# A two-layer decoder trunk: streamed sums placed more thinly in the first MLP, negated scores with an undivided first map, and one head-norm chain for both token tiles

## The chip, the core and the metric

One core of a Trainium2 chip runs the whole program. The metric is the device time of one execution in microseconds, as the median of three runs. The engines are named as the profile names them: PE is TensorE (PEld its weight loads), DVE is VectorE, ACT is ScalarE, POOL is GpSimd, SP is SyncE, whose queue issues the streamed loads.

## The reference, cut to what matters

A sequence of 256 tokens with 1024 features passes two layers, all in float32. Each layer is a token mixer and a squared-ReLU MLP with 4096 hidden columns; both are normed before, and shift, scale and gate of each norm come from a conditioning vector `c` (one product of `c` with a 1024 x 6144 matrix per layer). The mixer of layer 0 is native sparse attention (16 heads, three branches with gates), that of layer 1 is differential attention (8 heads with two maps each).

```python
cond = jax.nn.silu(c)
for i in range(DEPTH):
    mod = cond @ w_ada[i] + b_ada[i]
    sh1, sc1, g1, sh2, sc2, g2 = jnp.split(mod, 6, axis=-1)
    h = rms_norm(x, ln_mix_g[i]) * (1.0 + sc1[:, None, :]) + sh1[:, None, :]
    y = nsa_mixer(h, ...) if i % 2 == 0 else diff_mixer(h, ...)
    x = x + g1[:, None, :] * y
    h = rms_norm(x, ln_mlp_g[i]) * (1.0 + sc2[:, None, :]) + sh2[:, None, :]
    x = x + g2[:, None, :] * (jnp.square(jax.nn.relu(h @ w_mlp_in[i])) @ w_mlp_out[i])

# diff_mixer, for every head; q and k after a norm over 64 columns and a rotation of the first 16
q = apply_partial_rope(rms_norm(q, q_gain), cos, sin)
k = apply_partial_rope(rms_norm(k, k_gain), cos, sin)
s = jnp.einsum('bhcqd,bhckd->bhcqk', qb, k) * scale        # two maps c, scale = 1/8
p = masked_softmax(s, kpos[None, :] <= t[:, None])
a = p[:, :, 0] - lam * p[:, :, 1]
o = jnp.einsum('bhqk,bhkd->bhqd', a, v)
o = rms_norm(o, subln_g) * (1.0 - lam_init)                # over 128 columns
```

## The kernel before, in words

**Products.** Every large product is made of exactly split operands: `w = hi + lo`, both in float32r, and `mm3` (L79 to L83) adds hi.hi, hi.lo and lo.hi in one bank of 512 columns. A 256 x 1024 activation stands as two token tiles of 128.

**The weight stream.** Before anything is computed, the program writes two lists: `items` (raw buffers of 128 x 1024 floats, 524 KB each, loaded by SP in that order) and `units` (what is to be done with them). `plan` (L112) appends a unit of weights; `plan_ada` (L118) appends eight steps of a conditioning sum, one for each tile of 128 rows of the conditioning matrix. `do_unit` (L187) takes the units in their order. A weight unit is split: a cast for the high half (L199) on the engine that the table `halves` names for this turn, and a subtraction for the low half (L203) on the other. A conditioning step is one operation on VectorE over 1024 columns: a multiplication for the first of eight (L224), then a multiply-add (L229); with `with_pool` (second MLP only) VectorE multiplies (L226) and GpSimd adds (L227). `use` (L238) does the units up to the next weights and splits `look` units ahead; `issue` (L154) starts loads `ahead_dma` items ahead. Raw buffers, halves, sums and larger activations share one ring of 32 slots of 4 KB a partition (tag "w").

**Where the sums stand.** `plan_mlp` (L517) writes the units of an MLP with its extra steps: from the third block on one step behind every unit, until there are none. The first MLP carries 24 steps: its own gate, and shift and scale of the differential layer's norm. Shift and scale of the second MLP's norm, 16 steps, stand in the differential layer: `one_k` (L556) puts one behind each of the first 16 units of the projections q0, k1, q1 and v0. The second MLP carries 8 steps for its gate. After the eighth step `fin` folds a sum over partitions: `ada_cols` (L362) with four small products (L366), a copy, and, as an entry of the list `pend`, two transposes and a copy (L374, L376). `flush` (L183) runs all of `pend` at the next weight unit. `fin_gate` (L413) folds a gate by products at once.

**Head norms.** `head_norms` (L792) takes the two token tiles of a projection as they lie in their banks. For each tile: squares on ScalarE (L798), sums of 64 columns on VectorE (L800), then `rsqrt_mean` (L299): a small VectorE operation (L302), logarithm and exponential on ScalarE (L306, L307), and four small VectorE operations for a Newton step (L308 to L311). Then the multiplication (L811), the rotation `rope` (L782: two products L788, a difference L789, a sum L790), four transposes on TensorE (L826), and ScalarE's copies with the gain into the key tiles (L842) or the query tile (L849). It is a generator; at each `yield fill` `weave` (L252) puts `fill` units of the next projection's products behind it. In `kv_post` (L893) the two key kinds of the sparse layer go through it one after the other.

**Attention.** `mask_max` (L1005) adds a mask of 0 and a large negative number and takes the maximum in one VectorE operation (L1008). A small operation multiplies the maximum by -0.125 (L1023 in the sparse layer, L1349 in the other), and ScalarE takes `exp(0.125 s + bias)` with its sum (L1028, L1354). `combine` (L1357) of the differential layer divides: a reciprocal, the second one times -lambda, then for each token tile a scaling of the first map (L1361) and a multiply-add of the second (L1362). Transposes (L1368), values (L1375, L1377), a norm over 128 columns, transposes (L1390) and the split (L1392, L1393) follow, head by head, in the order that the string given to `heads` (L1397) spells out (L1430 to L1437).

**Order.** The program text gives an order, which the framework's scheduler may change engine by engine; the splits and the sums are issued with a lowered priority (`tc.high_priority(-50)`), and semaphores between the engines are set by the framework. So the rows of the orders below are what each engine's queue holds.

## Time and profile before

| | |
|---|---|
| median of three runs | 747.58 us (745.33 to 747.91) |
| span of the profiled execution (the page gives no other time for it) | 746.7 us |
| TensorE busy | 692.4 us (93%), 4263 products and transposes |
| VectorE busy | 505.6 us (68%) |
| ScalarE busy | 385.5 us (52%) |
| GpSimd busy | 233.5 us (31%) |
| read from memory | 154.86 MB, 209 GB/s over the span |

The program runs through stretches that the lines of the trace set apart: the start and first norm (0 to 62 us), the sparse layer (62 to 212, from 185 on mostly its output projection and the next norm), the first MLP (212 to 405), the differential layer (405 to 572, from 546 on mostly the end of its output projection and the next norm), the second MLP (572 to 747). Shares over the whole span mix these, so they are read stretch by stretch. A group of instructions is shown with its line, engine, operation, tiles (out<-in, partitions x elements), count, busy time and mean time of one.

### The profile page before, as it was taken

How to read it: one execution, taken by the hardware profiler on the slowest of the kernel's cores; microseconds unless marked ns; L12 is line 12 of the kernel's file. 1: busy time of each engine (PE TensorE's matmuls, PEld its weight loads, DVE VectorE, ACT ScalarE, POOL GpSimd, SP SyncE). 2: the span in 40 equal slices, each digit the busy share in tenths (PEclk: the TensorE clock that was granted, in tenths of full speed). 3: DMA queues.
4: the chain of work that ended last, by engine and by line, in shares of the span. 5: the costliest groups of instructions: out<-in, count | busy, mean ns of one | idle time of the engine just before them, and what ended most of it. 6: DMA issues, size and time to landing. Idle time of an engine off the chain costs nothing. (4 is left out here: it accounts for less than half of the span.)

```text
span 746.7 us, 11822 instructions
## 1 busy us (share of the span) xinstructions
PE 692.4 (93%) x4263; PEld 569.3 (76%) x4263; DVE 505.6 (68%) x1051; ACT 385.5 (52%) x780; POOL 233.5 (31%) x151
## 2 busy tenths in 40 slices
PE   8999799998889999999999978888889999999997
PEld 6788565665578988899885756566669879988896
DVE  4447989969766788764338969888777653326653
ACT  6555338667356345554447342666646365445540
POOL 4102800004222232232324413125322864223430
PEclk9999999999999999999999989899999999999999
DMA  9999999313636999965676776434383499565001
GB/s 292 333 337 358 321 296 270 117 57 119 198 107 197 329 312 334 350 208 186 200 246 232 257 225 224 148 104 117 111 281 112 145 314 331 173 206 183 5 1 57
DMA packets 105423, 156.70 MB, mean 210 GB/s; under 512 B 6135, under 2 KB 60180, under 8 KB 105364
## 3 DMA queue, kind: packets, MB, share of 16 engines
q1 hardware_dynamic: 103952, 153.60, 64.0%
q0 software_dynamic: 1248, 2.20, 1.0%
q8 instruction: 34, 0.56, 0.3%
q14 instruction: 25, 0.20, 0.1%
q10 hardware_dynamic: 164, 0.14, 0.1%
HBM read 154.86 MB, written 1.06 MB: 209 GB/s over the span
## 5 line engine op out<-in xcount | busy, mean ns | idle before, releaser
L203 POOL TENSOR_TENSOR wl<-wr,wh 128x1024 fp32r<-128x1024 f32 x66 | 171.1, 2593 | 371.7 <-ACT wh L199 273.4
L203 DVE TENSOR_TENSOR wl<-wr,wh 128x1024 fp32r<-128x1024 f32 x126 | 181.2, 1451 | 80.4 <-ACT wh L199 49.9
L199 ACT CAST wh<-wr 128x1024 fp32r<-128x1024 f32 (+1 forms) x175 | 174.9, 1029 | 51.5 <-POOL acc L227 16.1
L83 PE MATMUL acc<-wh,z 128*128 128x512 f32 (+1 forms) x320 | 126.5, 396 | 5.2 <-DVE z L77 4.7
L81 PE MATMUL acc<-wh,z 128*128 128x512 f32 (+1 forms) x320 | 127.9, 400 | 0.0
L82 PE MATMUL acc<-wl,z 128*128 128x512 f32 (+1 forms) x320 | 126.2, 394 | 0.0
L83 PE MATMUL sc<-hh,wl 128*128 128x256 f32 x384 | 108.9, 284 | 1.2 <-POOL wl L203 1.2
L81 PE MATMUL sc<-hh,wh 128*128 128x256 f32 x384 | 109.2, 284 | 0.0
L82 PE MATMUL sc<-hl,wh 128*128 128x256 f32 x384 | 108.8, 283 | 0.0
L81 PEld LDWEIGHTS sc<-hh,wh 128*128 128x128 f32 x384 | 73.7, 192 | 2.1 <-issue 1.2
L83 PEld LDWEIGHTS sc<-hh,wl 128*128 128x128 f32 x384 | 73.7, 192 | 1.4 <-POOL wl L203 1.4
L83 PEld LDWEIGHTS acc<-wh,z 128*128 128x128 f32 x320 | 60.5, 189 | 18.5 <-DVE z L77 5.6
L82 PEld LDWEIGHTS sc<-hl,wh 128*128 128x128 f32 x384 | 73.7, 192 | 0.5
L1199 ACT ACTIVATE t<-sc 128x512 f32<-128x512 f32 x32 | 19.1, 597 | 101.1 <-PE sc L83 101.0
L81 PEld LDWEIGHTS acc<-wh,z 128*128 128x128 f32 x320 | 60.7, 190 | 12.4 <-issue 0.9
L82 PEld LDWEIGHTS acc<-wl,z 128*128 128x128 f32 x320 | 60.6, 189 | 11.9 <-issue 0.7
L77 DVE TENSOR_TENSOR z<-t,z 128x512 fp32r<-128x512 f32 x24 | 24.5, 1020 | 66.6 <-ACT z L76 66.5
L81 PE MATMUL acc<-wh,hh 128*128 128x512 f32 (+1 forms) x160 | 66.2, 415 | 2.1 <-DVE qn L811 1.3
L229 DVE SCALAR_TENSOR_TENSOR acc<-wr,cond,acc 128x1024 f32<-128x1024 f32 x42 | 62.7, 1493 | 0.6
L83 PE MATMUL acc<-wh,hl 128*128 128x512 f32 (+1 forms) x160 | 62.3, 389 | 0.6 <-DVE hl L1161 0.6
L82 PE MATMUL acc<-wl,hh 128*128 128x512 f32 (+1 forms) x160 | 62.3, 389 | 0.5 <-DVE wl L203 0.5
L81 PE MATMUL sc<-wh,hh 128*128 128x256 f32 (+1 forms) x152 | 44.1, 292 | 1.4 <-DVE hh L1160 1.4
(292 smaller groups left out, 1202.5 us busy)
## 6 DMA issues: line engine op xcount, KB each, us to landing
wr<-in_w_ada_dram SPq DMA_DIRECT2D x80, 512.0 KB, 6.5
wr<-in_w_mlp_in_dram SPq DMA_DIRECT2D x64, 512.0 KB, 5.0
wr<-in_w_mlp_out_dram SPq DMA_DIRECT2D x64, 512.0 KB, 4.4
wr<-in_diff_w_in_dram SPq DMA_DIRECT2D x24, 512.0 KB, 4.9
wr<-in_w_ada_dram SPq DMA_DIRECT2D x32, 256.0 KB, 6.6
wr<-in_nsa_w_in_dram SPq DMA_DIRECT2D x16, 512.0 KB, 7.4
wr<-in_nsa_w_out_dram SPq DMA_DIRECT2D x16, 256.0 KB, 10.8
wr<-in_diff_w_out_dram SPq DMA_DIRECT2D x8, 512.0 KB, 3.6
```

What stands on the lines that cost most here:

```text
L77: vec.tensor_tensor(l, src, h.bitcast(F32), op=ALU.subtract)
L81: pe.matmul(out, x[0], w[0], start=start, stop=False, skip_group_check=True)
L82: pe.matmul(out, x[0], w[1], start=False, stop=False, skip_group_check=True)
L83: pe.matmul(out, x[1], w[0], start=False, stop=stop, skip_group_check=True)
L199: hi(h, r[:, 0:n])
L203: lo.tensor_tensor(l, r[:, 0:n], h.bitcast(F32), op=ALU.subtract)
L229: vec.scalar_tensor_tensor(st["acc"], r, c, st["acc"], op0=ALU.mult, op1=ALU.add)
L1199: act.activation(r, bk, AF.Relu)
```

## The change

1. *Sums.* `plan_mlp` gets a function `share(i)` that gives the steps behind unit i. The first MLP carries all 40 steps: its gate, and shift and scale of the next two norms, one behind each of three of four units from the tenth on (`i > 7` and `i % 4 > 0`, i from 0). The projections of the differential layer carry none. The second MLP has its 8 steps behind the units from the thirteenth on, one each.
2. *Folding.* Entries of `pend` have a count. `ada_cols` queues its products three weight units later and the transposes one unit after them; `fin_gate` is queued three units later too.
3. *Head norms.* One chain for both token tiles: the sums of squares go into one 128 x 16 tile, and `rsqrt_mean` and `rope` run once over both tiles; the multiplications stay one for each tile. The normed heads lie in one slot of the ring (`w4`) instead of two small tiles. In the sparse layer's `kv_post` the two key kinds go through one chain too, and the gate sums stand inside it. For keys of the differential layer the last of the three fills is two units instead of one.
4. *Negated scores.* The gains of the queries are multiplied by -0.125 once, so products of queries and keys are the negated, scaled scores; the mask is 0 and a large positive number, the operation takes the minimum, and the exponential is `exp(-s + min)`. The small operation in between is left out.
5. *Undivided first map.* `combine` leaves the first map as it is and adds the second times -lambda s0 / s1. Since a norm over columns follows, the factor s0 is left out but for EPS, which becomes EPS s0 s0.
6. *Halves.* In the differential layer all high halves are cast by ScalarE; every second low half is made by GpSimd, as before.

```diff
-    def flush():
-        while pend:
-            pend.pop(0)()
+    def flush(everything=True):
+        for e in pend:
+            e[0] -= 1
+        while pend and (everything or pend[0][0] <= 0):
+            pend.pop(0)[1]()
...
     def ada_cols(acc, then):
-        bk = bank()
...
+        def front():
+            bk = bank()
...
+            act.copy(row, bk[:, 0:256])
+            pend.insert(0, [1, lambda: back(row)])
...
-        pend.append(back)
+        pend.append([3, front])
...
-        return f
+        return lambda acc: pend.append([3, lambda: f(acc)])
...
+        for j in (0, 3):
+            vec.tensor_scalar(grot[:, j : j + 1], grot[:, j : j + 1], -0.125, None, op0=ALU.mult)
...
+    def head_norms(blocks, tabs, finish, perm=False, plain=None, fill=(1, 1, 1)):
+        ss = small([P, 2, 8], "hns")
+        q = w4("qn").rearrange("p (t h d) -> p t h d", t=2, h=8)
+        for t, hs, b in blocks:
+            n = hs.stop - hs.start
+            sq = tmp()[:, 0 : 64 * n]
             act.activation(sq, b, AF.Square)
-            ss = small([P, 8], "hns")[:, 0:nh]
-            vec.reduce_sum(ss, sq.rearrange("p (h d) -> p h d", d=64), axis=AX.X)
-            rs.append(rsqrt_mean(ss, 64, [P, nh], f"hn{nh}"))
-        yield fill
+            vec.reduce_sum(ss[:, t, hs], sq.rearrange("p (h d) -> p h d", d=64), axis=AX.X)
+        r = rsqrt_mean(ss.rearrange("p t h -> p (t h)"), 64, [P, 16], "hn").rearrange("p (t h) -> p t h", t=2)
+        yield fill[0]
...
+        rope(q, tabs)
+        yield fill[2]
+        heads_T(q, finish)
...
-    def mask_max(bks, pr, mx):
+    def mask_min(bks, pr, mn):
...
-                vec.tensor_tensor_reduce(pr[:, h, T2[t][1]], bk[:, h * w : (h + 1) * w], m, 1.0, -3e38, ALU.add, ALU.max,
-                                         mx(h, t))
+                vec.tensor_tensor_reduce(pr[:, h, T2[t][1]], bk[:, h * w : (h + 1) * w], m, 1.0, 3e38, ALU.add, ALU.min,
+                                         mn(h, t))
...
-    plan_mlp(0, [(0, 1, 2), (1, 0, 0), (1, 0, 1)])
+    plan_mlp(0, [(0, 1, 2), (1, 0, 0), (1, 0, 1), (1, 1, 0), (1, 1, 1)], lambda i: int(i % 4 > 0) if i > 7 else 0)
...
-        U["d" + nm, i] = plan_rows(w_dif, c0, [[one_k]] * 4)
+        U["d" + nm, i] = plan_rows(w_dif, c0)
...
-    plan_mlp(1, [(1, 1, 2, True)])
+    plan_mlp(1, [(1, 1, 2, True)], lambda i: int(i > 11))
...
-    halves[0] = [(vec.tensor_copy, pool), (act.copy, vec), (act.copy, pool), (act.copy, vec)]
+    halves[0] = [(act.copy, pool), (act.copy, vec)]
...
         def combine(s):
-            vec.reciprocal(s.sm, s.sm)
-            vec.tensor_scalar(s.sm[:, :, 1], s.sm[:, :, 1], nlam, None, op0=ALU.mult)
+            r, e = s.cf[:, 0], s.cf[:, 1]
+            vec.reciprocal(r, s.sm[:, 1])
+            vec.scalar_tensor_tensor(r, r, nlam, s.sm[:, 0], op0=ALU.mult, op1=ALU.mult)
+            vec.scalar_tensor_tensor(e, s.sm[:, 0], EPS, s.sm[:, 0], op0=ALU.mult, op1=ALU.mult)
             for t, sl in T2:
-                vec.tensor_scalar(s.pr[:, 0, sl], s.pr[:, 0, sl], s.sm[:, t, 0:1], None, op0=ALU.mult)
-                vec.scalar_tensor_tensor(s.pr[:, 0, sl], s.pr[:, 1, sl], s.sm[:, t, 1:2], s.pr[:, 0, sl],
+                vec.scalar_tensor_tensor(s.pr[:, 0, sl], s.pr[:, 1, sl], r[:, t : t + 1], s.pr[:, 0, sl],
                                          op0=ALU.mult, op1=ALU.add)
...
-    weave(head_norms(bk0, 4, 8, to_kz(4, kz[0:2])), gq)
+    weave(head_norms(rows8(bk0), [(slice(0, 8), 4)], to_kz((4, 4), kz[0:2]), fill=(1, 1, 2)), gq)
...
-    c[:, 264:392] = np.where(p[None, :] <= p[:, None], 0.0, NEG)
+    c[:, 264:392] = np.where(p[None, :] <= p[:, None], 0.0, -NEG)
```

What this does to the order of the queues is shown at three places. The first is VectorE at the first key norm of the differential layer; `hn8t`, `hn8r` and `hn8m` are the small tiles of the norm (`hnt`, `hnr`, `hnm` in the changed kernel), `wl` is the low half of a weight unit, `acc` of L229 a conditioning sum. Before:

```order
L229 SCALAR_TENSOR_TENSOR acc<-wr,cond,acc 128x1024
L310 TENSOR_SCALAR hn8t<-hn8t 128x8
L309 TENSOR_TENSOR hn8t<-hn8t,hn8m 128x8
L229 SCALAR_TENSOR_TENSOR acc<-wr,cond,acc 128x1024
L311 TENSOR_TENSOR hn8r<-hn8r,hn8t 128x8
L310 TENSOR_SCALAR hn8t<-hn8t 128x8
L229 SCALAR_TENSOR_TENSOR acc<-wr,cond,acc 128x1024
L311 TENSOR_TENSOR hn8r<-hn8r,hn8t 128x8
L811 TENSOR_TENSOR qn<-acc,hn8r 128x512 x2
L788 TENSOR_TENSOR ropeA<-qn,csg 128x128
L788 TENSOR_TENSOR ropeB<-qn,csg 128x128
L203 TENSOR_TENSOR wl<-wr,wh 128x1024
```

In the changed kernel:

```order
L805 TENSOR_REDUCE hns<-t 128x8
L305 TENSOR_SCALAR hnm<-hns 128x16
L308 TENSOR_TENSOR hnt<-hnr 128x16
L309 TENSOR_TENSOR hnt<-hnt,hnm 128x16
L310 TENSOR_SCALAR hnt<-hnt 128x16
L311 TENSOR_TENSOR hnr<-hnr,hnt 128x16
L814 TENSOR_TENSOR qn<-acc,hnr 128x512 x2
L781 TENSOR_TENSOR ropeA<-qn,csg 128x256
L781 TENSOR_TENSOR ropeB<-qn,csg 128x256
L206 TENSOR_TENSOR wl<-wr,wh 128x1024
L784 TENSOR_TENSOR qn<-ropeA,ropeB 128x16x8
L785 TENSOR_TENSOR qn<-ropeA,ropeB 128x16x8
```

The three conditioning sums that stood between the small operations are no longer in the queue, a norm has one chain of small operations instead of two interleaved ones, and the rotary products have 256 columns.

The second place is TensorE at the same norm, with buffer numbers: `acc_4571` and `acc_4572` are the two banks of the q0 projection, `acc_4728` and `acc_4729` those of k1, and L826 are the transposes behind the norm. Before:

```order
L82 MATMUL acc_4571<-wl_4509,hh_138 128x512
L826 MATMUL tr_4680<-first_75,qn_4622 128x128 x4
L83 MATMUL acc_4571<-wh_4508,hl_139 128x512
L81 MATMUL acc_4572<-wh_4508,hh_138 128x512
L82 MATMUL acc_4572<-wl_4509,hh_138 128x512
L83 MATMUL acc_4572<-wh_4508,hl_139 128x512
L81 MATMUL acc_4728<-wh_4603,hh_138 128x512
L82 MATMUL acc_4728<-wl_4604,hh_138 128x512
L83 MATMUL acc_4728<-wh_4603,hl_139 128x512
L81 MATMUL acc_4729<-wh_4603,hh_138 128x512
L82 MATMUL acc_4729<-wl_4604,hh_138 128x512
L826 MATMUL tr_4689<-first_75,qn_4624 128x128 x4
```

In the changed kernel `acc_4507` and `acc_4508` are the banks of q0, `acc_4623` and `acc_4624` those of k1, and the transposes are L793:

```order
L83 MATMUL acc_4507<-wh_4447,hl_139 128x512
L81 MATMUL acc_4508<-wh_4447,hh_138 128x512
L82 MATMUL acc_4508<-wl_4448,hh_138 128x512
L83 MATMUL acc_4508<-wh_4447,hl_139 128x512
L793 MATMUL tr_4603<-first_75,qn_4510 128x128 x4
L793 MATMUL tr_4612<-first_75,qn_4510 128x128 x4
L81 MATMUL acc_4623<-wh_4527,hh_138 128x512
L82 MATMUL acc_4623<-wl_4528,hh_138 128x512
L83 MATMUL acc_4623<-wh_4527,hl_139 128x512
L81 MATMUL acc_4624<-wh_4527,hh_138 128x512
```

The transposes of the first tile stood ahead of the last four products of q0, and those of the second tile behind five products of k1. Now all 48 products of q0 stand ahead, and the transposes of both tiles follow one another.

The third place is VectorE in the last blocks of the first MLP, where `z` is the low half of a hidden block (L77) and `acs` the folded columns of a sum. Before:

```order
L77 TENSOR_TENSOR z_3850<-t,z_3849 128x512
L203 TENSOR_TENSOR wl<-wr,wh 128x1024 x3
L77 TENSOR_TENSOR z_3850<-t,z_3849 128x512
L203 TENSOR_TENSOR wl<-wr,wh 128x1024 x2
L77 TENSOR_TENSOR z_4058<-t,z_4057 128x512
L203 TENSOR_TENSOR wl<-wr,wh 128x1024 x3
L77 TENSOR_TENSOR z_4058<-t,z_4057 128x512
```

In the changed kernel (L206 is the low half, L227 and L232 the conditioning steps, L378 the copy of the folded columns):

```order
L77 TENSOR_TENSOR z_3737<-t,z_3736 128x512
L206 TENSOR_TENSOR wl<-wr,wh 128x1024
L227 TENSOR_SCALAR acc<-wr,cond 128x1024
L77 TENSOR_TENSOR z_3737<-t,z_3736 128x512
L232 SCALAR_TENSOR_TENSOR acc<-wr,cond,acc 128x1024 x2
L378 COPY acs<-tr 128x2x4
L206 TENSOR_TENSOR wl<-wr,wh 128x1024
L387 TENSOR_TENSOR mB_136<-acs,bcol 128x8
L206 TENSOR_TENSOR wl<-wr,wh 128x1024
L232 SCALAR_TENSOR_TENSOR acc<-wr,cond,acc 128x1024 x4
L206 TENSOR_TENSOR wl<-wr,wh 128x1024
L232 SCALAR_TENSOR_TENSOR acc<-wr,cond,acc 128x1024
```

The steps for the second MLP's shift and scale stand between the low halves here.

## Rows read from the trace of the kernel before

**Rows 1.** Busy time by stretch (x: instructions)

```profile
core 0: us, PE busy (x) PEld busy (x) DVE busy (x) ACT busy (x) POOL busy (x), PEclk, DMA share, GB/s
...
62.00:100.00 38.00, 31.43 (x192) 23.88 (x191) 34.00 (x84) 16.59 (x45) 18.46 (x21) 0.96 1.06 318
100.00:185.00 85.00, 81.04 (x501) 50.25 (x500) 73.46 (x336) 58.32 (x195) 10.25 (x4) 0.98 0.57 162
...
212.00:405.00 193.00, 188.98 (x1223) 168.25 (x1223) 122.23 (x108) 94.85 (x129) 54.96 (x28) 0.99 0.75 251
405.00:480.00 75.00, 63.91 (x270) 47.63 (x271) 66.03 (x132) 33.34 (x71) 25.50 (x16) 0.91 0.65 217
480.00:546.00 66.00, 57.23 (x271) 42.09 (x269) 53.41 (x171) 40.50 (x129) 24.71 (x17) 0.97 0.38 116
...
572.00:747.00 175.00, 169.00 (x1076) 153.09 (x1074) 85.02 (x67) 79.10 (x99) 69.31 (x28) 1.00 0.47 157
```

**Rows 2.** Waits of TensorE, 405 to 546 us (total us, times, longest us)

```profile
PE tr L826 <- DVE qn L790: 10.9, 4, 4.2
PE tr L1368 <- DVE z L1393: 2.2, 2, 1.6
```

**Rows 3.** Timeline of TensorE, 430 to 436 us (start us, us, [idle before])

```profile
430.59 0.39 PE L81 MATMUL acc<-wh,hh 128*128 128x512 f32 x1
430.82 0.39 PE L82 MATMUL acc<-wl,hh 128*128 128x512 f32 x1
435.20 1.12 PE L826 MATMUL tr<-first,qn 128*128 128x128 f32 x4 [3.99 <-DVE qn L790]
```

**Rows 4.** Timeline of ScalarE and VectorE, 419 to 434 us

```profile
419.51 0.60 ACT L798 ACTIVATE t<-acc 128x512 f32<-128x512 f32 x1 [5.39 <-PE acc L83]
...
427.07 2.38 DVE L310 TENSOR_SCALAR hn8t<-hn8t 128x8 f32<-128x8 f32 x1
...
429.44 1.28 DVE L229 SCALAR_TENSOR_TENSOR acc<-wr,cond,acc 128x1024 f32<-128x1024 f32 x1
...
433.65 1.22 DVE L203 TENSOR_TENSOR wl<-wr,wh 128x1024 fp32r<-128x1024 f32 x1
```

**Rows 5.** Groups of VectorE, 408 to 546 us (busy us, mean ns)

```profile
L229 DVE SCALAR_TENSOR_TENSOR acc<-wr,cond,acc 128x1024 f32<-128x1024 f32 x14 | 20.1, 1436 | 0.0
...
L199 DVE CAST wh<-wr 128x1024 fp32r<-128x1024 f32 x8 | 5.5, 687 | 0.0
...
L811 DVE TENSOR_TENSOR qn<-acc,hn8r 128x512 f32<-128x512 f32 x8 | 5.2, 681 | 0.0
...
L1361 DVE TENSOR_SCALAR pr<-pr,dsm 128x128 f32<-128x128 f32 x8 | 4.0, 501 | 0.0
...
L1361 DVE TENSOR_SCALAR pr<-pr,dsm 128x256 f32<-128x256 f32 x8 | 2.8, 347 | 0.0
...
L788 DVE TENSOR_TENSOR ropeB<-qn,csg 128x128 f32<-128x128 f32 x8 | 2.3, 286 | 0.0
```

**Rows 6.** Groups of ScalarE, 408 to 546 us

```profile
L842 ACT ACTIVATE kz<-tr,grot 64x256 f32<-64x256 f32 x16 | 7.5, 469 | 24.1 <-PE tr L826 23.9
```

**Rows 7.** Groups of VectorE, 100 to 185 us

```profile
L1023 DVE TENSOR_SCALAR nb<-mx 128x4 f32<-128x4 f32 x16 | 4.9, 307 | 0.1
...
L1034 DVE TENSOR_TENSOR sm<-sm,gates 128x4 f32<-128x4 f32 x16 | 2.6, 161 | 0.1
...
L986 DVE TENSOR_TENSOR t<-t,csm 128x256 f32<-128x256 f32 x2 | 0.8, 425 | 0.0
```

**Rows 8.** Waits of TensorE, 62 to 212 us

```profile
PE tr L826 <- DVE qn L790: 3.8, 3, 3.3
```

**Rows 9.** Busy time by stretch, two of the first MLP

```profile
245.00:305.00 60.00, 59.11 (x394) 53.40 (x393) 49.29 (x37) 25.48 (x32) 17.05 (x10) 1.00 0.95 330
320.00:380.00 60.00, 60.00 (x402) 55.58 (x401) 28.34 (x20) 30.68 (x39) 18.75 (x8) 1.00 0.62 194
```

**Rows 10.** Waits of TensorE, 212 to 405 us

```profile
PE tr L366 <- DVE acc L229: 1.7, 2, 0.9
```

157 lines of the change are left out of this document (69 added, 88 removed).

## Prediction

> **What bounds the kernel now.** I read the stretches first [rows 1]. In the first MLP (212 to 405 us) TensorE is busy 188.98 of 193 us and in the second (572 to 747) 169.00 of 175: both are bound by products, and only fewer waits can shorten them. In the differential layer (405 to 546) it is busy 63.91 of 75 and 57.23 of 66 us, so it idles 19.9 us, and the granted clock is 0.91 and 0.97. With the two levels 1.2 and 2.4 GHz, 0.91 over 75 us means 13.5 us at the lower one and 0.97 over 66 us 4.0 us; at half speed that is 17.5 / 2 = 8.7 us of lost products. VectorE is the busiest of the other engines there: 66.03 of 75 us. In the sparse layer TensorE idles 6.6 us from 62 to 100 and 4.0 us from 100 to 185, while VectorE is busy 34.00 of 38 and 73.46 of 85.
>
> Then for whom TensorE waits in the differential layer [rows 2]: 10.9 us in four waits of the transposes behind a head norm, for VectorE's rotary result; the next largest is 2.2 us. The timeline shows the first of the four [rows 3]: a GEMM starts at 430.82, the transposes at 435.20, after 3.99 us of idle time. VectorE was not idle meanwhile [rows 4]: between the small operations of the chain stand conditioning sums (L229, 1.28 us), low halves of weights (L203, 1.22), and one operation on 8 columns that took 2.38 us. So TensorE is held by VectorE's queue at the four head norms, and behind such a wait the clock is low.
>
> **The change, part by part.** The sum is made against the profiled execution, span 746.7 us; the median of the runs is 747.58, 0.9 more.
>
> *Sums out of the differential layer.* Sixteen steps leave VectorE there, at 1.436 us [rows 5] 23 us. The order of the changed kernel has none between the parts of a chain.
>
> *Split casts.* The 8 casts on VectorE, 5.5 us [rows 5], go to ScalarE.
>
> *One chain for two tiles.* Per norm five small operations instead of ten, 20 fewer in the layer at some 0.16 us (a small one of four columns in [rows 7]): 3.2 us. The two reductions and the two multiplications stay. A rotary product on 256 columns does not occur before; it lies between 0.286 us (128 columns [rows 5]) and twice that. I take 0.425, another 256 column operation [rows 7], so 8 of them replace 16 for 1.2 us less; the rotary sums alike, 1.
>
> *Undivided first map.* Sixteen scalings go, 4.0 + 2.8 us [rows 5]; one small operation per head comes, 8 at 0.16: 5.5 us less.
>
> *Negated scores.* The small operation between a mask and its exponentials goes: 16 times in the sparse layer, 4.9 us [rows 7], and 8 times here, by the same mean 2.4 us.
>
> Together VectorE loses some 42 of the 119.4 us that it works between 405 and 546 [rows 1]. For the first long wait, step by step: the square of the second tile starts at 419.51 and takes 0.60 [rows 4], so it ends at 420.1. Behind it come in the new order two additions to the gate and one reduction on 512 columns (0.68 each, as the multiplication in [rows 5]), one small operation (0.16), two on ScalarE (0.2 each, an estimate from the same small one), four small ones (0.64), two multiplications (1.36), two rotary products (0.85), one low half (1.22) and two rotary sums (0.57, as the 128 column product): 7.2 us, and with 0.1 us for each of eight hand-overs 8.0, so 428.1. TensorE gets to these transposes at 430.82 plus the four GEMMs of the q projection that now stand ahead, at a pitch of 0.23 [rows 3]: 431.7. The wait is gone with 3.6 us to spare. In the next chain ScalarE has eight key writes of 0.469 us [rows 6] ahead of the logarithm and the chain takes some 9.0 us, while 36 GEMMs (8.3) and eight transposes (1.1, half of the slow-clock duration in [rows 3] for each four) are ahead on TensorE: 9.4, just covered. The third chain has 48 GEMMs ahead and no key writes before it.
>
> So I take all 10.9 us of this wait, 3 of the other 9.0 us of idle time and 7 of the 8.7 us of slow clock: 20.9 us. The ends are 11 (half of it, if something else ends the chains) and 19.9 + 8.7 = 28.6 (all of it).
>
> A point against this stands in [rows 4]: the operation on 8 columns took 2.38 us instead of 0.16 beside a low half on GpSimd, and GpSimd keeps every second low half. I leave it inside the margins. The Trainium skill, "SBUF — State Buffer", section "SBUF: two separate sides", says that VectorE and GpSimd share a port pair under an exclusive lock held for a whole instruction, and that VectorE operations with two SBUF inputs need it as well. The 2.38 us agree. By that rule the rotary products can be held too, the second chain's margin goes, and the layer would give some 16 instead of 21 us; this is part of the first rival.
>
> *The sums in the first MLP.* 40 steps behind three of four units from the tenth on, instead of 24 behind every unit of a shorter stretch. VectorE has 193 - 122.23 = 70.8 us free there [rows 1] and gets 23 more. In the dense stretch of before, one sum per unit, TensorE worked 59.11 of 60 us [rows 9], so a thinner one costs nothing, covered by that free time; without it the low halves, which stand in the same queue, would be late by a sum each. The small products that fold two results into columns move along: what they cost here they save there, zero.
>
> *The queued folding.* Three units later it no longer waits for the last sum: 1.7 us in the first MLP [rows 10]. For the one gate of the second MLP I take 0.6; its ends are 0 and the 0.9 us that the longest of the waits in [rows 10] took.
>
> *Sparse layer.* The two chains of the keys become one; the transposes behind norms wait 3.8 us now [rows 8]; I take 3. Between 100 and 185 us VectorE loses 4.9 us of bias operations and some 5 more of small ones, but TensorE is busy 81.04 of 85 us: 3 of its 4.0 idle us is all I take. Sum 6, ends 0 and 11 (the length follows VectorE's 9.9, and 1 of the keys).
>
> *Buffers.* The normalized heads take a slot of the weight ring. The DMA share is 0.38 to 0.65 in the differential layer [rows 1], so a transfer that starts later is hidden: 0, ends 0 and 1 us.
>
> Sum: 20.9 + 1.7 + 0.6 + 6 = 29.2 us, 746.7 - 29.2 = 717.5, and with the 0.9 us of the median 718.4. A measurement of this kernel can tell some 0.5% (3.7 us) from no change.
>
> **The rivals.**
> 1. *The chains still end late, on ScalarE or beside GpSimd.* For it: logarithm and exponential queue behind key writes and casts, ScalarE gets 8 casts more, and the second chain has 0.4 us of margin. Against it: ScalarE works only 73.8 of the 141 us [rows 1]. Price: three of the four waits come back with 2 us each, and 6 us of the clock: 12 us. 730.
> 2. *VectorE sets the sparse layer's length too*, and the differential layer gives all its idle time: 28.6 + 11 + 2.3 = 42. 705.6. For it: 73.46 of 85 us; against: TensorE's 81.04.
> 3. *Nothing to see.* The waits move on to the head pipeline behind the norms, whose exponentials nothing here shortens, and the layers together give below 4 us: 743 to 748. Against it: the pipeline's largest wait is 2.2 us in [rows 2].
> 4. *Slower: the weights of the first MLP come late.* In the calm stretch the queue moves 194 GB/s for one unit after the other; three more transfers for four units make that 1.75 x 194 = 340, and the dense stretch moved 330 at a DMA share of 0.95 [rows 9]. Over 53 units, some 143 us at the calm stretch's 2.7 us for 524 KB, this is 48.6 MB, of which 14 transfers (7.3 MB) run ahead. TensorE begins to wait if less than 41.3 MB come in 143 us, 289 GB/s, and the change loses on the whole from 41.3 MB in 172 us on, 240 GB/s. At 225 it would lose 41 us: 759. Against it: 318 to 330 GB/s wherever so much was asked for [rows 1, 9].
>
> **How the numbers follow.** Forecast 0.52 (712 to 725), rival 1 0.21 (725 to 738), rival 2 0.15 (703 to 712), rival 3 0.06, rival 4 0.04, faster than all of these 0.02. The predicted time is the forecast's. The range of 8 in 10 takes in the bulk of rival 2 and of rival 1: low 746.7 - 42 = 705; high 746.7 - 11 (the layer's low end) + 0.9 = 737. Slower by over 0.5% is rival 4 and a rest of rival 3: 0.05; within 0.5% the rest of rival 3: 0.05; faster 0.90.
>
> **What the profile of after would show.** If right: no wait of the transposes behind a head norm above 1 us in the differential layer, a granted clock of 0.98 or more there, VectorE some 40 us less busy, and the layer some 21 us shorter; the first MLP as long as before within 3 us, at over 300 GB/s for most of it; the sparse layer about 6 us shorter. Rival 1 if these transposes still wait, with ScalarE's logarithm and exponential late; rival 4 if the first MLP is longer and its high halves wait for transfers. If VectorE's time in the layer falls by 40 us and the layer's length by less than 8, the cause that I give for the waits is wrong.

## The result, and the profile after

The changed kernel takes 736.71 us (median of four runs, 734.79 to 737.27) against 747.11 for the kernel before on the same chip; the ratio is 0.9853 with a 95% interval of 0.9825 to 0.988. It is faster by 10.4 us, where 29.2 were forecast. The profiled execution has a span of 735.1 us, 11.6 less than that of before.

To see where the rest is, each profile is cut at the first transposes of the three later norms (L1148 before, L1150 after), which TensorE reaches as soon as the layer ahead gives it a normed tile. They start at 202.0, 397.8 and 551.8 us before and at 200.5, 397.8 and 533.0 after. Below, a kernel's **four stretches** are always these: start and sparse layer, first MLP, differential layer, second MLP.

| us | start and sparse | first MLP | differential | second MLP |
|---|---|---|---|---|
| before | 202.0 | 195.8 | 154.0 | 194.9 |
| after | 200.5 | 197.3 | 135.2 | 202.1 |
| difference | -1.5 | +1.5 | -18.8 | +7.2 |
| forecast | -6 | -1.7 | -20.9 | -0.6 |

The layer that the change was made for gave nearly what was forecast. The second MLP, whose code hardly changed, took back 7.2 us, and the sparse layer gave a quarter of its term.

The engines in these four stretches, before:

```profile
core 0: us, PE busy (x) PEld busy (x) DVE busy (x) ACT busy (x) POOL busy (x), PEclk, DMA share, GB/s
0.00:202.00 202.00, 182.96 (x1227) 131.56 (x1228) 149.14 (x528) 113.67 (x308) 49.05 (x59) 0.97 0.82 246
202.00:397.80 195.80, 188.57 (x1213) 170.09 (x1213) 124.26 (x113) 97.12 (x134) 54.46 (x26) 0.99 0.75 250
397.80:551.80 154.00, 133.16 (x610) 97.17 (x610) 130.18 (x319) 81.56 (x215) 56.61 (x36) 0.94 0.55 180
551.80:746.70 194.90, 187.72 (x1214) 170.49 (x1214) 102.01 (x94) 93.16 (x126) 73.38 (x30) 1.00 0.47 155
```

And after:

```profile
0.00:200.50 200.50, 182.91 (x1228) 132.78 (x1228) 139.40 (x451) 114.70 (x300) 46.36 (x59) 0.98 0.82 248
200.50:397.80 197.30, 190.22 (x1233) 170.15 (x1233) 146.71 (x134) 96.25 (x134) 57.77 (x26) 0.99 0.83 288
397.80:533.00 135.20, 123.24 (x590) 92.77 (x590) 105.61 (x238) 88.44 (x214) 53.69 (x36) 1.00 0.43 142
533.00:735.10 202.10, 192.15 (x1214) 174.43 (x1214) 102.34 (x94) 93.15 (x126) 73.33 (x30) 0.97 0.46 153
```

The windows of [rows 1] from the first MLP on, after:

```profile
core 0: us, PE busy (x) PEld busy (x) DVE busy (x) ACT busy (x) POOL busy (x), PEclk, DMA share, GB/s
...
212.00:405.00 193.00, 190.14 (x1248) 167.55 (x1247) 140.82 (x127) 92.58 (x129) 55.68 (x26) 1.00 0.85 296
405.00:480.00 75.00, 68.05 (x308) 52.98 (x307) 62.08 (x117) 49.03 (x99) 32.35 (x20) 1.00 0.35 116
480.00:546.00 66.00, 57.66 (x294) 44.02 (x293) 49.18 (x130) 43.19 (x124) 24.15 (x17) 1.00 0.51 168
546.00:572.00 26.00, 26.00 (x193) 25.06 (x193) 16.27 (x18) 14.29 (x21) 8.21 (x4) 0.94 0.43 139
572.00:735.00 163.00, 156.48 (x964) 141.23 (x962) 74.80 (x59) 69.91 (x86) 61.27 (x25) 0.97 0.45 149
```

Three things stand out. In the differential stretch VectorE executes 81 instructions fewer and is busy 105.6 us instead of 130.2: 24.6 less, where some 42 were forecast. (The window from 405 to 546 us shows only 8 less, 111.3 instead of 119.4, but after the change it ends 13 us into the second MLP's stretch.) In the start and sparse stretch VectorE loses 9.7 us, as forecast, but TensorE's idle time there falls only from 19.0 to 17.6 us. And the clock, now full in the differential layer, falls behind it, in the second MLP (0.94, 0.97), where it was 1.00 before: with the same 1214 instructions TensorE is busy 4.4 us longer there, and it idles 2.8 us longer.

The durations of VectorE's records in the differential stretch add up to 153.1 us before and 117.8 after, 35.3 less. The busy time falls by less, since neighbouring records overlap: before, a small operation between others that do not need it takes 0.08 us of the queue and not its 0.16:

```profile
425.72 0.15 DVE L309 TENSOR_TENSOR hn8t<-hn8t,hn8m 128x8 f32<-128x8 f32 x1
425.80 0.16 DVE L308 TENSOR_TENSOR hn8t<-hn8r 128x8 f32<-128x8 f32 x1
425.87 1.28 DVE L229 SCALAR_TENSOR_TENSOR acc<-wr,cond,acc 128x1024 f32<-128x1024 f32 x1
```

In the merged chain, where each small operation needs the one before, they start 0.21 us apart.

The waits of TensorE after, from 405 to 546 us; the first line answers to [rows 2]:

```profile
PE tr L793 <- DVE qn L785: 3.3, 4, 1.9
...
PE sc L83 <- DVE hl L1163: 2.4, 2, 1.8
```

The transposes behind a head norm wait 3.3 instead of 10.9 us. The second line is new in its size (these waits were 0.6 us before): the low half `hl` of the activation that the second MLP starts with. VectorE and GpSimd at that place, in the timeline:

```profile
540.62 1.22 DVE L206 TENSOR_TENSOR wl<-wr,wh 128x1024 fp32r<-128x1024 f32 x1
...
542.02 2.37 POOL L206 TENSOR_TENSOR wl<-wr,wh 128x1024 fp32r<-128x1024 f32 x1 [1.84 <-ACT wh L202]
...
542.41 2.53 DVE L1163 TENSOR_TENSOR hl<-t,hh 128x512 fp32r<-128x512 f32 x1
...
546.84 0.68 DVE L1163 TENSOR_TENSOR hl<-t,hh 128x512 fp32r<-128x512 f32 x1
```

The same operation takes 0.68 us at 546.84 and 2.53 at 542.41, where GpSimd had begun a low half 0.4 us earlier: it ends 0.55 us after GpSimd's does. Before, VectorE made `hl` ahead of a weight's low half instead of behind it, and was done with `hl` when GpSimd began:

```profile
560.42 0.69 DVE L1161 TENSOR_TENSOR hl<-t,hh 128x512 fp32r<-128x512 f32 x1
...
561.03 1.22 DVE L203 TENSOR_TENSOR wl<-wr,wh 128x1024 fp32r<-128x1024 f32 x1
...
561.77 2.73 POOL L203 TENSOR_TENSOR wl<-wr,wh 128x1024 fp32r<-128x1024 f32 x1 [1.78 <-ACT wh L199]
```

At the first head norm, where [rows 4] stand for before, low halves and rotary products do the same:

```profile
417.64 6.04 DVE L206 TENSOR_TENSOR wl<-wr,wh 128x1024 fp32r<-128x1024 f32 x2 [0.64 <-issue]
...
427.24 4.94 POOL L206 TENSOR_TENSOR wl<-wr,wh 128x1024 fp32r<-128x1024 f32 x2 [4.65 <-DMA wr<-in_diff_w_in_dram]
428.36 1.57 DVE L781 TENSOR_TENSOR ropeA<-qn,csg 128x256 f32<-128x256 f32 x1
429.85 2.61 DVE L781 TENSOR_TENSOR ropeB<-qn,csg 128x256 f32<-128x256 f32 x1
```

Two low halves take 6.04 us, where 1.22 each was usual. The forecast had the rotary products at 0.425 us each, and the transposes ready at 428.1; they start at 434.06. I call such a stretched operation **held**. Counted over the profile (each form's durations beside a GpSimd operation of 1024 columns, less the median of the same form elsewhere), holds add up to some 80 us in either profile, of VectorE's 494 us after and 506 before. This is an estimate: it is 80 to 85 us after and 71 to 83 before, by how often a form must have run elsewhere to be counted.

The last place is in the second MLP, where GpSimd adds up the gate's steps:

```profile
568.53 19.86 POOL L230 TENSOR_TENSOR acc<-acc,wr 128x1024 f32<-128x1024 f32 x7 [0.69 <-DVE acc L227]
...
588.35 2.34 POOL L206 TENSOR_TENSOR wl<-wr,wh 128x1024 fp32r<-128x1024 f32 x1
...
590.75 0.58 PE L83 MATMUL sc<-hh,wl 128*128 128x256 f32 x1 [2.70 <-POOL wl L206]
```

A low half stands behind seven additions, and TensorE waits 2.70 us for it (before, 1.2 us at this place, with 0.6 us for the gate's folding just ahead). This is no hold of VectorE: the low half is late in GpSimd's own queue. Behind the wait the clock is at its lower level, 0.50 from 590 to 595 us:

```profile
585.00:590.00 5.00, 3.04 (x26) 2.84 (x24) 0.50 (x1) 1.57 (x2) 4.92 (x3) 1.00 0.96 339
590.00:595.00 5.00, 4.25 (x20) 4.25 (x21) 4.36 (x4) 4.06 (x6) 2.43 (x2) 0.50 0.90 298
```

### The profile page after: what moved, and what is told of

Same layout as the page of the kernel before. It is cut to its first block, busy times and chain, and to the rows that moved or that the text cites. A ratio compares the mean times of both kernels' runs of the same rounds, so it can differ in the third digit from the quotient of the medians.

```text
span 735.1 us, 11670 instructions
## 1 busy us (share of the span) xinstructions
PE 688.5 (94%) x4263; PEld 570.1 (78%) x4263; DVE 494.1 (67%) x914; ACT 392.5 (53%) x770; POOL 231.1 (31%) x151
## 4 chain that ended last, share of the span: by engine, by line
PE 59%; DVE 16%; issue 10%; POOL 6%; ACT 4%; DMA 4%; SPq 1%; POOLq 0%; ACTq 0%; DVEq 0%
PE acc L83 9%; PE acc L82 9%; PE acc L81 8%; PE sc L83 8%; PE sc L81 8%; PE sc L82 8%; DVE wl L206 4%; POOL acc L230 3%; DMA wr<-in_nsa_w_in_dram 2%; ACT wh L202 2%; PE sc L1007 1%; DVE pr L1042 1%; PE tr L172 1%; SPq L158 1%; POOL wl L206 1%
## 5 line engine op out<-in xcount | busy, mean ns | idle before, releaser
L206 POOL TENSOR_TENSOR wl<-wr,wh 128x1024 fp32r<-128x1024 f32 x66 | 169.5, 2571 | 365.2 <-ACT wh L202 263.2
L206 DVE TENSOR_TENSOR wl<-wr,wh 128x1024 fp32r<-128x1024 f32 x126 | 182.8, 1465 | 72.5 <-ACT wh L202 50.4
L202 ACT CAST wh<-wr 128x1024 fp32r<-128x1024 f32 (+1 forms) x183 | 182.5, 1029 | 57.6 <-POOL acc L230 16.1
L77 DVE TENSOR_TENSOR z<-t,z 128x512 fp32r<-128x512 f32 x24 | 26.7, 1112 | 59.3 <-ACT z L76 59.3
L81 PE MATMUL acc<-wh,hh 128*128 128x512 f32 (+1 forms) x160 | 62.4, 393 | 0.0
L232 DVE SCALAR_TENSOR_TENSOR acc<-wr,cond,acc 128x1024 f32<-128x1024 f32 x42 | 61.5, 1464 | 0.6
L82 PE MATMUL acc<-wl,hh 128*128 128x512 f32 (+1 forms) x160 | 60.1, 376 | 1.7 <-POOL wl L206 1.0
L83 PE MATMUL acc<-wh,hl 128*128 128x512 f32 (+1 forms) x160 | 59.6, 372 | 0.0
```

Of the source, the lines that this page charges most:

```text
L77: vec.tensor_tensor(l, src, h.bitcast(F32), op=ALU.subtract)
L81: pe.matmul(out, x[0], w[0], start=start, stop=False, skip_group_check=True)
L82: pe.matmul(out, x[0], w[1], start=False, stop=False, skip_group_check=True)
L83: pe.matmul(out, x[1], w[0], start=False, stop=stop, skip_group_check=True)
L202: hi(h, r[:, 0:n])
L206: lo.tensor_tensor(l, r[:, 0:n], h.bitcast(F32), op=ALU.subtract)
```

## The experiments

All results in one table; the ratio is to the kernel before, run beside each on the same chip (746.3 to 747.9 us). All are edits to the changed kernel unless "before" is named.

| | us | ratio, 95% interval | stretches |
|---|---|---|---|
| after | 736.7 | 0.9853, 0.9825 to 0.988 | 200.5, 197.3, 135.2, 202.1 |
| e1 sums back | 744.4 | 0.9978, 0.9955 to 1.0002 | 201.2, 196.6, 149.1, 200.7 |
| e2 before, sums moved | 739.3 | 0.989, 0.9862 to 0.9918 | 202.0, 197.0, 144.3, 195.0 |
| e3 gate on VectorE | 733.6 | 0.9822, 0.98 to 0.9844 | 200.2, 197.4, 135.2, 198.4 |
| e4 one low half | 734.2 | 0.9826, 0.9803 to 0.985 | 202.0, 197.3, 135.3, 198.7 |
| e5 e3 and e4 | 730.8 | 0.9772, 0.9745 to 0.9798 | 198.8, 197.3, 135.2, 195.0 |
| e6 two key chains | 737.3 | 0.9866, 0.984 to 0.9893 | 200.3, 197.3, 135.3, 202.1 |
| e7 split chains | 738.0 | 0.9879, 0.9848 to 0.9909 | 200.0, 197.3, 138.9, 199.4 |
| e8 no GpSimd halves, differential | 728.2 | 0.9733, 0.9711 to 0.9755 | 200.2, 197.5, 128.5, 200.4 |
| e9 e5 and e8 | 723.5 | 0.9664, 0.9631 to 0.9698 | 200.3, 198.4, 128.6, 194.7 |
| e10 none anywhere | 708.4 | 0.9469, 0.9434 to 0.9505 | 193.7, 190.8, 128.1, 192.8 |
| e11 before, none in differential | 735.5 | 0.9832, 0.9795 to 0.9869 | 202.2, 194.3, 140.6, 195.5 |
| e12 none in sparse | 727.2 | 0.9713, 0.9664 to 0.9763 | 196.0, 195.3, 134.9, 199.4 |
| e13 before, none anywhere | 717.4 | 0.9603, 0.9588 to 0.9617 | 194.9, 188.3, 139.0, 192.8 |
| e14 e10, sums back | 709.5 | 0.9494, 0.9478 to 0.951 | 193.9, 189.2, 132.1, 192.6 |

The span of e1's profile, 747.6 us, lies high among its runs (742.96 to 749.6). Each row of stretches is from one profile, and a stretch varies. The start and sparse stretch has the same code in the changed kernel and in e1, e3, e4, e5, e7, e8 and e9, and takes 198.8 to 202.0 us. The second MLP has the same code in the changed kernel and in e1, e6, e7, e8 and e12, with the same waits of 1.8 and 2.7 us, and takes 199.4 to 202.1, at a granted clock of 0.99 to 0.97. So a difference of up to 3 us in one of these two stretches shows nothing by itself.

### What the parts of the change give (e1, e2, e7)

e1 leaves the two parts out of the first MLP's list and restores `one_k`:

```diff
-    plan_mlp(0, [(0, 1, 2), (1, 0, 0), (1, 0, 1), (1, 1, 0), (1, 1, 1)], lambda i: ...
+    plan_mlp(0, [(0, 1, 2), (1, 0, 0), (1, 0, 1)], lambda i: ...
...
-        U["d" + nm, i] = plan_rows(w_dif, c0)
+        U["d" + nm, i] = plan_rows(w_dif, c0, [[one_k]] * 4)
```

> The changed kernel with only the 16 sums for the second MLP's norm put back behind the units of q0, k1, q1 and v0 in the differential layer. A stretch is counted from the first transposes of the norm ahead of it to those of the next: the differential layer's is 154.0 us before and 135.2 after. Theory (VectorE's queue holds TensorE at the head norms, and the sums are 23 of the 42 us that leave it): the stretch goes up by about 12 us to 147, the waits of the transposes behind a head norm come back to 6 us or more, and the time is about 747. Rival (the merged chain and the undivided map gave the gain, and the sums only filled free time): the stretch stays below 140 us and the time below 741.

e2 is the kernel before with the new `plan_mlp` and its two calls, and without `one_k`.

> The kernel before with only the order of the sums changed: all 40 in the first MLP, behind three of four units, none in the differential layer; head norms, masks, maps and folding as before. Theory: the stretch of the differential layer falls from 154.0 to 142 to 144 us, the first MLP's grows by 1 to 2 us for the moved folding products, and the time is 736 to 739. Rival: the stretch stays at 150 or more, the time at 744 or more.

e7 calls `rsqrt_mean` and `rope` once for each tile in the differential layer:

```diff
+            rr = [rsqrt_mean(ss[:, t], 64, [P, 8], "hn8") for t in range(2)]
...
+        for sl in (slice(0, 1), slice(1, 2)) if dif else (slice(0, 2),):
+            rope(q, tabs, sl)
```

> The changed kernel with the head norms of the differential layer done tile by tile again (two chains of small operations, rotary products of 128 columns), but with the transposes of both tiles together and all products of the next projection's first three units ahead of them, as in the changed kernel. Theory (what takes time in VectorE's queue are the sums and GpSimd's holds; the merged chain gives what its 20 small operations cost, 3 to 5 us of VectorE, of which TensorE sees a part): the differential stretch grows from 135.2 to 137 to 139 us, the time to 738 to 740. Rival (the merged chain is the main part of the 9 us that the rest gave): the stretch grows by 6 us or more.

e1's stretch grows to 149.1 us, more than the theory's 147, and three of the waits are back, though the time is below the theory's 747:

```profile
PE tr L798 <- DVE qn L790: 7.8, 3, 4.2
```

e2 comes out just above its theory's bounds, at 144.3 and 739.3 us. In the differential stretch the moved sums alone give 9.7 us (e2), all the rest alone 4.9 (e1), both together 18.8: each is worth some 4 us more with the other. That supports the theory of e1 and e2 in size, but not its simple form. In e2 the sums are gone, and the transposes (L813 there) still wait 8.6 us of the 10.9 in [rows 2]:

```profile
PE tr L813 <- DVE qn L777: 8.6, 3, 4.9
```

Something else in VectorE's queue kept the norms late. The merged chain was worth 3.7 us of the stretch (e7), as expected, and 1.3 of the time, since the second MLP was 2.7 shorter there, at the same waits and a clock of 0.99; the intervals of the ratios overlap.

### The second MLP (e3, e4, e5)

```diff
-    plan_mlp(1, [(1, 1, 2, True)], lambda i: int(i > 11))
+    plan_mlp(1, [(1, 1, 2)], lambda i: int(i > 11))
```

> The changed kernel with the sums of the last gate done by VectorE alone (one multiply-add for each step) instead of a product on VectorE and an addition on GpSimd. In the changed kernel seven additions hold GpSimd for 19.9 us, a low half stands behind them, TensorE waits 2.7 us for it at 588 us, and its clock is 0.50 for some 7 us after. Theory (the second MLP lost 7.2 us partly here): that wait and that fall of the clock go, the second MLP's stretch falls from 202.1 to 197 to 199 us, and the time by 3 to 5 us to 732 to 734. Rival (VectorE gets 7 times 0.5 us more and its low halves come late instead): no change beyond 1 us.

```diff
-                    lo.tensor_tensor(l, r[:, 0:n], h.bitcast(F32), op=ALU.subtract)
+                    (vec if u == U["up", 1, 1, 1][0] else lo).tensor_tensor(l, r[:, 0:n], h.bitcast(F32), op=ALU.subtract)
```

> The changed kernel with one single low half moved from GpSimd to VectorE: that of the first unit of the second hidden block in the second MLP's upper half, which GpSimd worked on from 542.02 to 544.39 us while VectorE's low half of the normed activation took 2.53 us instead of 0.68. Theory (GpSimd's operation holds VectorE's, and the late operand costs TensorE a wait and its clock): the operation takes 0.7 us, the wait of 1.8 us and the fall of the clock at 546 to 550 go, and the time falls by 3 to 4 us to 733. Rival (VectorE's queue is late there by itself, and gets 1.2 us more): no change, or 1 us slower.

e5 has both edits.

> The changed kernel with both edits to the second MLP: the last gate summed by VectorE alone, and the one low half beside the norm moved from GpSimd to VectorE. Theory (two separate places, each a late operand and a fall of the clock): the gains add, 736.7 - 3.1 - 2.5 = 731, the second MLP's stretch is 195 to 196 us as before the change, and no fall of the clock is left in it. Rival (the two share one cause, so the second edit gains nothing behind the first): 733 to 734.

Each edit takes away its wait (e3 brings a new one of 1.6 us, for `z`), and the gains add: 3.1, 2.5, and 5.9 us together. Alone, neither gain is clear of noise (the intervals of the ratios overlap that of the changed kernel), and e4's is below its theory's 3 to 4 us; together they are clear. The second MLP's stretch is back at 195.0, that of before. In e4 GpSimd does nothing beside the low half of the activation:

```profile
543.96 0.68 DVE L1163 TENSOR_TENSOR hl<-t,hh 128x512 fp32r<-128x512 f32 x1
```

The granted clock from 530 to 550 us is 1.00 there, and from 585 to 600 it is still 0.77, since the additions remain; in e3 it is the other way round, 0.91 and 1.00. So the loss had two places, both GpSimd's, both in operations that the change did not edit. At the first, VectorE reached `hl` while GpSimd was at a low half. Before, a product of the gate's (L226) met it, which took 2.26 us instead of 0.75 and for which TensorE did not wait.

The shorter layer is not what brought `hl` there. e1's layer is only 4.9 us shorter than that of before, and its rows are the same:

```profile
555.87 2.37 POOL L206 TENSOR_TENSOR wl<-wr,wh 128x1024 fp32r<-128x1024 f32 x1 [1.84 <-ACT wh L202]
...
556.26 2.53 DVE L1168 TENSOR_TENSOR hl<-t,hh 128x512 fp32r<-128x512 f32 x1
```

The wait stands in every kernel that has the change and this low half on GpSimd, with layers of 128.5 to 149.1 us. It does not stand in e2, the kernel before with the new order of the sums (layer 144.3, second MLP 195.0). What differs is the order in VectorE's queue, `hl` behind the weight's low half; which of the parts 2 to 6 of the change sets it, no run shows.

### GpSimd and VectorE (e8, e9, e10, e11)

```diff
-    halves[0] = [(act.copy, pool), (act.copy, vec)]
+    halves[0] = [(act.copy, vec)]
```

> The changed kernel with no low half on GpSimd in the differential layer: all on VectorE. VectorE gets 16 times 1.22 = 19.5 us more there, and loses what GpSimd's operations held: the rotary products of 256 columns took 0.41 us where GpSimd was idle and 1.45 to 2.62 us beside a low half, 8.6 us in the four norms. Theory (holds): all eight rotary products at 0.41 to 0.43 us, VectorE's busy time in the layer up by 8 us or less instead of 19.5, the differential stretch within 2 us of 135.2. Rival (the long rotary products are slow by themselves, for their columns or their pattern): they stay at 1.4 us or more, and the stretch grows by 5 us or more.

The holds are what the theory said, and the gain is larger. The eight rotary products of the four norms take 0.42 us each. The differential stretch in e8, to be read against the one after the change (135.20 us, VectorE 105.61):

```profile
397.70:526.20 128.50, 123.00 (x591) 93.11 (x591) 100.92 (x254) 88.04 (x214) 14.12 (x20) 1.00 0.48 153
```

VectorE does 16 instructions more in e8, the low halves at 1.22 us, and is busy 4.7 us less; GpSimd is free of 39.6 us. What GpSimd took off VectorE it had taken back as holds, and more, at moments that the program did not choose. In the changed kernel the list of TensorE's waits has none that ended with GpSimd in this stretch, so GpSimd's own slowness (2.41 us for a low half, in the median) is not what cost time here. The stretch falls by another 6.7 us, the time by 8.5.

e9 joins the edits of e8 and e5.

> The changed kernel with three edits: no low half on GpSimd in the differential layer, the last gate summed by VectorE alone, and the one low half beside the second MLP's norm on VectorE. Theory (the gains of 8.5, 3.1 and 2.5 us lie in separate places and add): 722 to 724 us, the differential stretch 128 to 129 us, the second MLP's 195 to 197. Rival (the second MLP's wait comes from the phase in which the layer ends, so the edits to it do nothing behind a shorter layer): 726 to 728.

The theory held: 723.5 us. e10 makes every low half on VectorE (`pool` becomes `vec` in all tables of `halves`) and has the gate as in e3.

> The changed kernel with no low half on GpSimd anywhere (66 of them to VectorE) and the last gate summed by VectorE alone. Theory (what GpSimd takes from VectorE's queue it gives back as holds, also in the sparse layer and in the MLPs): 718 to 722 us, no slower than the three edits alone; VectorE's busy time up by much less than 66 times 1.22 = 80 us. Rival (in the first MLP, where VectorE has 140.8 of 193 us to do, 22 more low halves make it the bound): the first MLP's stretch grows by 3 us or more beyond 197.3.

708.4 us, 28 less than the changed kernel and better than the theory said; the rival is out, as the first MLP's stretch shrinks to 190.8. The groups of VectorE's low halves, after and then e10:

```profile
L206 DVE TENSOR_TENSOR wl<-wr,wh 128x1024 fp32r<-128x1024 f32 x126 | 182.8, 1465 | 72.5 <-ACT wh L202 50.4 <-POOL wl L206 13.1 <-issue 3.4
```

```profile
L206 DVE TENSOR_TENSOR wl<-wr,wh 128x1024 fp32r<-128x1024 f32 x192 | 226.3, 1201 | 63.3 <-ACT wh L202 61.8
```

192 instead of 126, at 1201 ns instead of 1465. The engines' totals, after and then e10:

```profile
PE 688.5 (94%) x4263; PEld 570.1 (78%) x4263; DVE 494.1 (67%) x914; ACT 392.5 (53%) x770; POOL 231.1 (31%) x151
```

```profile
PE 680.8 (97%) x4263; PEld 563.9 (80%) x4263; DVE 484.2 (69%) x980; ACT 391.5 (56%) x770; POOL 40.1 (6%) x78
```

VectorE does 66 operations more and is busy 10 us less. Part of this gain is not holds: TensorE's own waits for GpSimd, 6.0 us in the changed kernel, are gone too.

e11 makes the replacement of e8 in the kernel before.

> The kernel before with one edit: the low halves that GpSimd makes in the differential layer go to VectorE; sums, norms, masks and maps as before. Theory (VectorE's queue holds TensorE at the norms, and GpSimd's operations hold VectorE about as long as its own low half takes): the stretch falls from 154.0 to 147 to 150 us, the time to 740 to 743. Rival (VectorE is full there with the sums, and 16 low halves more make the chains later): the stretch grows, the time is 748 or more.

One edit to a table gives the kernel before 12.4 us (747.9 to 735.5), with all its sums, chains and maps in place; as much as the whole change within the intervals. Its differential stretch is 140.6, below the theory's 147.

### The sparse layer (e6, e12)

e6 norms the two key kinds of `kv_post` by two calls of `head_norms` with four heads each.

> The changed kernel with the two key kinds of the sparse layer normed one after the other again (each still with both token tiles in one chain), the gate sums behind them. In the changed kernel the compression's products started 3.7 us earlier, but waited 2.5 us for GpSimd's products, and the first scores came 1.8 us later than before. Theory (ahead of the scores other work sets the pace, so the merged key chain gives nothing there): the first scores within 1.5 us of 112.3 us and the time within 1.5 us of the changed kernel's. Rival (the merged chain did give its 3 us and something else took 5): the scores at 114 to 116 us, the time 2 to 4 us longer.

The theory held: the first scores come at 112.19 us, after 112.27 in the changed kernel, and the time is the same. The merged key chain gives nothing that shows; in eight profiles with the changed kernel's code there the first scores come at 110.6 to 113.7 us. e12 makes the replacement of e8 in the sparse layer's table.

> The changed kernel with no low half on GpSimd in the sparse layer (10 of them to VectorE, which also makes them for the norm ahead of the first MLP). Theory (the merged key chain gave nothing there because GpSimd, with a low half from 73.2 to 75.6 us ahead of its products for the compression, and its hold of VectorE before the first MLP's norm, are late next): the first scores 2 us earlier than 112.3, the wait of 4.2 us for the normed activation at 208 us below 2, the time 3 to 5 us less than the changed kernel's. Rival (loads and TensorE's own products set the sparse layer's length): within 1 us of it.

The theory held in direction, and the gain was twice its size, 9.5 us (the trace has 9 low halves of 1024 columns fewer on GpSimd). The first scores come at 110.30, which is hardly earlier than e5's 110.62 without this edit; from there to the next norm it takes 85.7 us instead of the 88.2 to 88.3 of all eight profiles, which is clear. The wait of 4.2 us for the normed activation is 1.4. Of the 9.5 us, 4.5 lie in the sparse stretch, 2.0 in the first MLP's, where this wait stands, and 2.7 in the second's:

```profile
526.20:725.60 199.40, 189.41 (x1214) 171.84 (x1214) 102.43 (x94) 93.18 (x126) 73.39 (x30) 0.99 0.48 154
```

There the waits of 1.8 and 2.7 us stand as in the changed kernel, and only the clock differs (0.99 for 0.97). e7, without an edit to the sparse layer, has the same 199.4, so these 2.7 us are not put down to the edit.

### What the change is worth without holds (e13, e14)

e13 is the kernel before with e10's edits, e14 is e10 with e1's.

> The kernel before with no low half on GpSimd anywhere and the last gate summed by VectorE alone: what the kernel of 708.4 us has, without the change. It shows what the change is worth where GpSimd holds nothing. Theory (the forecast's sum left out that GpSimd's operations take VectorE's time back, and their places; without them the change gives more than the 10.4 us measured, but less than the 29.2 forecast, since the edits to this kernel already gave 12 us in the layer): 722 to 727 us, so that the change gives 14 to 19. Rival A (the gain does not depend on GpSimd): 717 to 720. Rival B (the forecast's sum was right but for the holds): 735 or more.

> The kernel of 708.4 us (no low half on GpSimd, the gate on VectorE) with the 16 sums put back into the differential layer. Put back beside GpSimd's low halves they cost 13.9 us of the layer's stretch (135.2 to 149.1). Theory (VectorE's queue is what holds TensorE at the norms, and it is 18 us shorter without the holds, so the sums find more room): the stretch grows from 128.1 by 4 to 9 us, the time is 711 to 716. Rival (a sum between two small operations of a chain delays it whatever else the queue holds): the stretch grows by 12 us or more, the time is 719 or more.

My theory of e13 fell, and rival A held: without holds the change is worth 717.4 - 708.4 = 9.0 us, hardly another number than 10.4. But it is made of other parts: by stretches -1.2, +2.5, -10.9 and 0.0 us. The second MLP comes out near its forecast; the sparse layer and the first MLP do not. The sums, put back, cost 13.9 us of the differential stretch beside GpSimd's low halves (e1) and 4.0 without (e14), at the low end of e14's theory, and 1.1 us of the time (709.5, below the theory's 711), as the first MLP is shorter by 1.6; the intervals of e10 and e14 overlap. (VectorE is busy 99.6 us in e10's differential stretch, 6.0 less than after the change and not the 18 that the theory took.) So the sums, more than half of the 42 us that VectorE was to lose, had most of their price from the holds.

## Why the prediction was wrong

- **That head norms held TensorE through VectorE's queue** was right: the layer gave 18.8 of the 20.9 us forecast for it, and the clock from 405 to 546 us went from 0.91 and 0.97 to 1.00, as said. Its working was not. VectorE lost 24.6 us in the layer's stretch instead of 42, and TensorE 8.9 us of idle time there instead of 13.9; the rest is 9.9 us of TensorE's busy time, by the clock and 20 folding instructions less, where 7 were forecast for the clock. That so much less relief gave nearly the whole gain is luck. Two errors are in the 42. It is a sum of durations, and these do fall by 35.3 us, but the busy time by less, since neighbouring records overlap. And the eight rotary products took 12.0 us, where the sixteen of before had taken 4.6 and 1.2 less was forecast. The first chain was forecast to end at 428.1 and ended at 434.0: two low halves from 417.64 on took 6.04 us instead of 2.4, and the two rotary products 4.2 (1.57 + 2.61) instead of 0.85. Of the 5.9 us by which it was late, the margin of 3.6 and TensorE's own 0.4 left a wait of 1.9, so that "no wait above 1 us" failed too.
- **The step that failed** is "I leave it inside the margins", said of the small operation that took 2.38 us beside a low half on GpSimd in [rows 4]. The forecast took that row as one event of 2 us of the head norms; the profile of before holds some 80 us of the same, all over the program. Of the 17.6 us by which the four stretches fell short of the forecast, 7.8 are the second MLP's, 4.5 the sparse layer's, 3.2 the first MLP's and 2.1 the differential layer's. What was left out accounts for the first, where two waits for GpSimd made the loss (e3 to e5), and for the wait that is left in the layer. It does not account for the sparse layer and the first MLP, whose terms failed without holds too (e13 against e10) and are taken up below. The rule named with it (the Trainium skill, "SBUF — State Buffer", section "SBUF: two separate sides") speaks of an exclusive lock of a port pair for a whole instruction; the traces agree for the operations that read two operands from SBUF, such as the rotary products and low halves. The operation in [rows 4] reads a single SBUF tensor, so it shows a hold, but not one of two operands. The time landed in the band of rival 1, which had this mechanism; but rival 1 took its 12 us from three waits and the clock of the differential layer, where one wait above 1 us came and the clock was full, so that is luck.
- **The second MLP**: forecast -0.6, measured +7.2. I priced it as if nothing that the change does not edit could move. It lost to two places of GpSimd's (e3, e4): a changed order in VectorE's queue brought `hl` beside a low half on GpSimd, and TensorE waited 1.5 us longer for a low half behind GpSimd's additions (why longer, no run shows). No rival had it; rival 4 looked for a loss in the first MLP, where the transfers kept up (296 GB/s, DMA share 0.85, and +1.5 us).
- **The sparse layer**: forecast -6, measured -1.5. The term that failed is the 3 us of the keys. The wait of 3.8 us in [rows 8] did shrink, to 1.5 in one, but the compression's products then waited 2.3 us for GpSimd, and e6 shows that the merged chain moved nothing there: the first scores came at 112.3 us instead of 110.5, within what profiles of the same code differ by. The other 3 us, of the pairs, came: from the first scores to the first transposes of the next norm it takes 88.2 instead of 91.5 us.
- **The first MLP**: forecast -1.7, measured +1.5. I had the folding products cost zero, since they move along. TensorE is busy 1.65 us longer in this stretch (188.57 to 190.22), with 16 folding products and four transposes more; what they save lies in the differential stretch. The 1.7 us of waits in [rows 10] are gone, but TensorE idles as long as before (7.1 us against 7.2), among others 4.2 us for the normed activation at 208 us.

## What to carry to other kernels

Before a queue is relieved, compare each form's longest with its shortest duration: an operation that takes 0.4 us here and 2.6 there is held, and the engine that holds it is the first thing to move. Work given to GpSimd is not free for VectorE; here 66 low halves taken back cost VectorE no busy time and gave 28 us together with the gate. A sum of durations is not yet a sum of busy time, since short operations overlap their neighbours. And a forecast for one layer needs a line for each later stretch: here a new order in VectorE's queue and a late low half on GpSimd made most of 7 us in a stretch whose own code hardly changed.

## What was not expected of the hardware

Of VectorE's operations on SBUF that met a GpSimd operation of 1024 columns in the changed kernel, 53 were stretched by more than 0.3 us, and each ended after GpSimd's by less than its own usual duration: low halves took 1.22 us (median) elsewhere and 2.24 beside one, `z` in the MLPs (128 x 512) 0.69 and 2.47, the rotary products 0.42 and 1.5 to 2.6. One that reads a single SBUF tensor, the multiplication by a column (L227), took 0.75 and 2.52. It goes both ways: 15 of GpSimd's 66 low halves took more than 2.6 us; each of them had begun while a low half or a multiply-add ran on VectorE, and ended 2.2 to 2.3 us behind an operation of VectorE's that it met. The forms that read PSUM were not stretched at all: the masks with their minimum (L1013, nine of them beside GpSimd) 0.42 and 0.42, the scaled heads (L1390, ten) 0.35 and 0.35. And the price is as large as the work: with 66 low halves more (80 us at 1.2) VectorE was busy 10 us less, so GpSimd's 66 low halves and 7 additions had cost it some 90 us by this estimate, 1.2 each.
